# Expert weights by consecutive matrix rows per partition, in chunks of w1 or of w3 alone

## The chip, the cores and the metric

The kernel runs on one core of one Trainium2 chip. The metric is the device time of one execution in microseconds (us). Engines are named as the profile names them: PE is the TensorE matmul, PEld its weight load (the operand that stays in the array), DVE is VectorE, ACT is ScalarE, POOL is GpSimd, SP is SyncE, which here only issues DMAs; SPq and PEq are the sequencers of SP and PE.

## The reference, cut to what matters

An encoder of two layers on 512 tokens of width 1024. Each layer has a mixer (attention in layer 0, a gated recurrence in layer 1), a layer norm, a mixture of 16 experts with two of them chosen per token, and a second layer norm. What the change touches is the mixture:

```
for e in range(16):                       # w1, w3: [16, 1024, 512], w2: [16, 512, 1024], float32
    h = silu(t @ w1[e]) * (t @ w3[e])
    y = y + gates[:, e:e+1] * (h @ w2[e])
```

## The kernel before

**Tiling.** Each expert takes up to 96 tokens (`CAP`). Their rows are gathered from `hbuf` in HBM into `xg` [96, 1024] by an indirect DMA of POOL, two tiles in turn. `x_t` (lines 558 to 569) transposes `xg` on PE by eight blocks of 128 columns; ACT rounds the result to a high part `H` and DVE subtracts for the low part `L`. `w13` (571 to 589) multiplies with w1 and w3 into two PSUM tiles, 48 matmuls of 128x96 by 128x512: for each of the eight blocks `kc` of the contraction the products H·wh, H·wl and L·wh for w1 and for w3, mixed. `glu` (591 to 596) makes `hm` = silu(p1) * p3, with the silu on ACT and the product on DVE. `h_t` (598 to 606) transposes `hm` by four blocks, `w2` (608 to 629) does 24 matmuls, and `scatter` (631 to 638) adds the gated rows to `ybuf` in HBM by an indirect DMA.

**Weights.** Every weight is read from HBM as float32, in chunks of 1 MB, [128, 2048] floats, into rings of tiles named raw, rf, rr and rx (13 tiles while the experts run). A chunk has two parts of 1024 columns. Lines 133 and 134 turn a part into two tiles: ACT casts `wh` = round(w) and DVE subtracts `wl` = w - wh. Such pairs have 6 buffers while the experts run and 4 from the last expert's first part on (line 270). `Stream` (142 to 183) keeps the order: `conv_to(n)` emits conversions up to part n, and the loads before them. `expert_items` (666 to 690) makes the chunks of an expert: four for w1 and w3, each with 256 rows of w1 and the same 256 rows of w3 by two DMAs of 512 KB, and two for w2, of 256 rows each. Row a*128+p of a chunk goes to partition p, so a partition receives two separate rows per DMA, of 2 KB for w1 and w3 and of 4 KB for w2. SP issues all of them.

**Order.** `jobs` (692) runs w13 of expert e and then w2 of expert e-1; `x_t` of expert e+1 stands between them and `h_t` of expert e behind w2. Experts with more than 96 tokens put the rest into blocks of an overflow stage, `overflow` (815 to 834), behind w13 of expert 13, inside a branch whose condition all engines read first. In the profiled execution layer 0 has no such block and layer 1 has one (its tiles end in o: xto, p1o). The last expert's result goes through `direct` and `tail`. Instructions of an engine run in the order in which the program lists them; the framework may move an instruction ahead of others when it builds that list.

Of the kernel before, what the change touches and what calls it, by code (L numbers as in the profile page):

```python
# [8 lines left out]
F32 = mybir.dt.float32  # L9
# [10 lines left out]
P = 128  # L20
D = 1024
KC = D // P
# [6 lines left out]
CAP = 96  # L29
# [20 lines left out]
HALF = 1024  # L50
# [28 lines left out]
def host_consts():  # L79
    c = {}  # L80
    iota1 = np.broadcast_to(np.arange(1, P + 1, dtype=np.float32), (P, P))
    upper = np.triu(np.ones((P, P), np.float32), 1)
    w4 = np.broadcast_to(G - np.arange(G, dtype=np.float32), (P, G))
    tok = np.arange(P, dtype=np.float32)[:, None] + P * np.arange(NT, dtype=np.float32)[None, :]
    ix = np.broadcast_to(np.arange(XBLK, dtype=np.float32), (P, XBLK))
    tm = tok - OOB
    dump = S + np.arange(P, dtype=np.float32)[:, None]
    c["c_h"] = np.concatenate([iota1, upper, tm], 1).astype(np.float16)
    rel = np.arange(-P, P + 1)
    dist = np.abs(rel)  # L90
    far = 7 + sum((dist >= t).astype(np.int64) for t in (8, 12, 16, 23, 32, 46, 64, 91))
    bucket = np.where(rel > 0, 16, 0) + np.where(dist < 8, dist, far)
    rel = (np.arange(32)[:, None] == bucket[None]).astype(np.float32)
    inv = (np.float32(10000.0) ** (-np.arange(16, dtype=np.float32) / np.float32(16))).astype(np.float32)
    ang = np.arange(S, dtype=np.float32)[None, :] * inv[:, None]
    co, si = np.cos(ang), np.sin(ang)
    c["c_rot"] = np.ascontiguousarray(
        np.stack([np.tile(np.concatenate(x, 0), (4, 1)) for x in ((co, co), (-si, si))], 1).astype(np.float32))
    c["c_rel"] = rel
    c["c_sm"] = np.concatenate([np.eye(P, dtype=np.float32), w4, ix, tm, dump], 1).astype(np.float32)  # L100
    return c


def layout(I):
    """The inputs as the kernel loads them: slices, copies and permutations of what came in, and constants."""
    c = host_consts()
    a = {n: np.ascontiguousarray(I[n]) for n in _INS}
    rows = lambda x, n: np.broadcast_to(np.asarray(x).reshape(1, n), (P, n))
    vecs = [np.asarray(I[n]).reshape(-1, P).T for n in VECS]
    rw = np.asarray(I["router_w"]).reshape(KC, P, E).transpose(1, 0, 2).reshape(P, KC * E)  # L110
    a["c_all"] = np.ascontiguousarray(
        np.concatenate([c["c_sm"], rw, rows(I["router_bias"], E), rows(I["l0_sinks"], 8)] + vecs, 1))
    a["c_rel"] = np.ascontiguousarray(np.concatenate([c["c_rel"], np.asarray(I["rel_bias"])], 1))
    a["c_rot"], a["c_h"] = c["c_rot"], c["c_h"]
    a["xt"] = np.ascontiguousarray(np.asarray(I["x"])[0].T)
    w = np.asarray(I["l0_w_in"])
    a["lat"] = np.ascontiguousarray(np.concatenate([w[:, 256:416], w[:, 400:416], w[:, 384:400]], 1))
    a["ukv"] = np.ascontiguousarray(np.asarray(I["l0_w_ukv"]).reshape(P, 8, 2, 64).transpose(0, 2, 1, 3).reshape(P, 1024))
    uq = np.asarray(I["l0_w_uq"]).reshape(2, P, 2, 4, 96)
    uq = np.concatenate([uq[..., a_:z_].reshape(2, P, 2, -1) for a_, z_ in ((0, 64), (64, 96))] +  # L120
                        [np.concatenate([uq[..., 80:96], uq[..., 64:80]], -1).reshape(2, P, 2, -1)], -1)
    a["uq"] = np.ascontiguousarray(uq.transpose(1, 2, 0, 3).reshape(P, 2 * HALF))
    g = np.stack([np.asarray(I["l1_" + n]) for n in ("wa_f", "wx_f", "wa_b", "wx_b")])
    a["gates"] = np.ascontiguousarray(g.reshape(4, 4, 2, P, P).transpose(1, 3, 0, 2, 4).reshape(4, P, HALF))
    return a
# [73 lines left out]
class K:  # L199
# [358 lines left out]
    def x_t(self, xg, nm):  # L558
        nc = self.nc
        H = self.wp.tile([P, KC, CAP], F32R, name="xh" + nm, tag="xh", bufs=1)  # L560
        L = self.wp.tile([P, KC, CAP], F32R, name="xl" + nm, tag="xl", bufs=1)
        for q in range(2):
            pt = self.ps.tile([P, 4, CAP], F32, name=f"xt{nm}{q}", tag="t")
            for j in range(4):
                kc = 4 * q + j
                nc.tensor.transpose(pt[:, j], xg[:, kc * P:(kc + 1) * P], self.ident[:CAP, :CAP])  # L566
            nc.scalar.copy(H[:, 4 * q:4 * q + 4], pt)  # L567
            nc.vector.tensor_tensor(L[:, 4 * q:4 * q + 4], pt, H[:, 4 * q:4 * q + 4].bitcast(F32), op=ALU.subtract)
        return H, L

    def w13(self, st, key, H, L, nm, la):
        nc = self.nc
        p1, p3 = (self.ps.tile([P, 512], F32, name=x + nm, tag="h", bufs=4)[:CAP] for x in ("p1", "p3"))
        for i in range(4):
            a = st.where[(key, "a", i)]
            st.conv_to(a + 2 + la)
            w1h, w1l = st.get(a)
            w3h, w3l = st.get(a + 1)
            for j in range(2):
                kc = 2 * i + j  # L580
                sl = slice(j * 512, (j + 1) * 512)
                f, e = kc == 0, kc == KC - 1
                nc.tensor.matmul(p1, H[:, kc], w1h[:, sl], start=f, stop=False)  # L583
                nc.tensor.matmul(p1, H[:, kc], w1l[:, sl], start=False, stop=False)  # L584
                nc.tensor.matmul(p3, H[:, kc], w3h[:, sl], start=f, stop=False)  # L585
                nc.tensor.matmul(p3, H[:, kc], w3l[:, sl], start=False, stop=False)  # L586
                nc.tensor.matmul(p1, L[:, kc], w1h[:, sl], start=False, stop=e)  # L587
                self.last_mm = nc.tensor.matmul(p3, L[:, kc], w3h[:, sl], start=False, stop=e).ins  # L588
        return p1, p3

    def glu(self, p1, p3, nm):
        nc = self.nc
# [5 lines left out]
    def h_t(self, hm, nm, tag="h"):  # L598
        nc = self.nc
        H, L = (self.wp.tile([P, FC, CAP], F32R, name=f"h{x}{nm}", tag=tag + x, bufs=1) for x in "hl")  # L600
        pt = self.ps.tile([P, FC, CAP], F32, name=f"ht{nm}", tag="t")
        for j in range(FC):
            nc.tensor.transpose(pt[:, j], hm[:, j * P:(j + 1) * P], self.ident[:CAP, :CAP])
        nc.scalar.copy(H, pt)
        nc.vector.tensor_tensor(L, pt, H.bitcast(F32), op=ALU.subtract)  # L605
        return H, L
# [59 lines left out]
    def expert_items(self, it, l, e, what, key):  # L666
        I, nc = self.I, self.nc

        def rows(name, r, n):
            src = I[f"l{l}_{name}"][e] if isinstance(e, int) else \  # L670
                I[f"l{l}_{name}"][bass.ds(e, 1)].rearrange("o a b -> (o a) b")
            return src[r:r + n].rearrange("(a p) b -> p a b", p=P)

        def ld_a(c):
            def load(t):
                for i, n in enumerate(("w1", "w3")):
                    nc.sync.dma_start(t[:, i * HALF:(i + 1) * HALF].rearrange("p (a b) -> p a b", a=2),
                                      rows(n, c * 256, 256))
            return load

        def ld_b(c):
            def load(t):
                nc.sync.dma_start(t.rearrange("p (a b) -> p a b", a=2), rows("w2", c * 256, 256))
            return load

        for c in range(4 if what == "a" else 2):
            if what == "a":
                it.add((key, "a", c), ld_a(c))
            else:
                it.add((key, "w2", c), ld_b(c))  # L690
# [1030 lines left out]
```

## Time and profile before

| | |
|---|---|
| Time, median of 3 runs | 1189.37 us (1189.37 to 1190.99) |
| Profiled execution, first to last instruction (its span) | 1188.6 us |
| PE busy | 1056.6 us (89%) |
| DVE busy | 953.0 us (80%) |
| ACT busy | 768.1 us (65%) |
| Mean granted TensorE clock | 0.937 of full speed |

The profile has no time of its own beside its span; the timed runs stand 0.8 us above it, which is taken as what lies around the span. A busy time is the union of an engine's instructions, and matmuls overlap: one lasts 0.39 us while the next starts 0.23 us after it. So distances between starts say more than durations. The experts run from about 280 to 590 us in layer 0 and from about 841 to 1166 us in layer 1.

### The profile page before, as it was taken

Reading aid. Unit: us, or ns where it says so; the run is one execution under the profiler, and the core shown is the slowest. Engines: PE = TensorE matmul, PEld = TensorE weight load, DVE = VectorE, ACT = ScalarE, POOL = GpSimd, SP = SyncE. Lnnn points to the kernel's source line nnn. Section 1 sums busy time; section 2 is a strip of 40 time slices with the busy share of each in tenths; the row PEclk is TensorE's granted clock in tenths of the full one; section 3 lists DMA queues with packets and bytes.
Section 4 is the critical chain, followed back from the end, with each engine's and each line's share of the span. In section 5 each row is a group of like instructions: output and inputs, shape, how many; then the busy total and the mean of one; then the engine's idle time right before and its main releaser. Section 6 shows DMA issues by size and latency. Waiting matters only on the chain. (4 is left out here: it accounts for less than half of the span.)

```text
span 1188.6 us, 15070 instructions
## 1 busy us (share of the span) xinstructions
PE 1056.6 (89%) x5042; PEld 783.3 (66%) x5042; DVE 953.0 (80%) x1487; ACT 768.1 (65%) x1114; POOL 318.2 (27%) x278
## 2 busy tenths in 40 slices
PE   8999889986999999989789768797799999999892
PEld 6677677874777777756478546586577777776651
DVE  5685878367999999967767999947899998996785
ACT  5455778225788788757526665533578888876762
POOL 1112555125131121111234536203422211210122
PEclk9897999996999999989979969798799999999996
DMA  8180010877999999988713112295799999996983
GB/s 288 54 260 21 2 36 18 335 263 263 324 348 371 360 365 355 345 295 300 188 55 106 35 54 72 87 365 206 269 335 336 380 374 367 387 332 204 335 268 108
DMA packets 132693, 281.25 MB, mean 237 GB/s; under 512 B 8872, under 2 KB 32584, under 8 KB 132480
## 3 DMA queue, kind: packets, MB, share of 16 engines
q1 hardware_dynamic: 121344, 245.20, 56.8%
q0 software_dynamic: 10928, 33.93, 11.9%
q10 hardware_dynamic: 336, 1.08, 0.2%
q8 instruction: 42, 0.69, 0.2%
q14 instruction: 43, 0.35, 0.1%
HBM read 261.41 MB, written 23.74 MB: 240 GB/s over the span
## 5 line engine op out<-in xcount | busy, mean ns | idle before, releaser
L134 DVE TENSOR_TENSOR wl<-rr,wh 128x1024 fp32r<-128x1024 f32 x180 | 212.2, 1218 | 20.9 <-ACT wh L133 20.1
L133 ACT CAST wh<-rr 128x1024 fp32r<-128x1024 f32 x180 | 180.2, 1049 | 39.6 <-PE p L587 34.1
L134 DVE TENSOR_TENSOR wl<-rf,wh 128x1024 fp32r<-128x1024 f32 x104 | 123.8, 1219 | 17.5 <-ACT wh L133 17.3
L133 ACT CAST wh<-rf 128x1024 fp32r<-128x1024 f32 x104 | 105.2, 1048 | 43.4 <-PE p L587 15.1
L134 DVE TENSOR_TENSOR wl<-raw,wh 128x1024 fp32r<-128x1024 f32 (+1 forms) x97 | 116.1, 1225 | 20.2 <-ACT wh L133 11.6
L133 ACT CAST wh<-raw 128x1024 fp32r<-128x1024 f32 (+1 forms) x93 | 92.8, 1031 | 25.5 <-PE p L587 6.0
L636 POOL DMA_INDIRECT ybuf<-y,dst x30 | 57.2, 1907 | 185.7 <-ACT y L635 175.4
L625 PE MATMUL py<-wh,hh 128*96 128x512 f32 x256 | 102.9, 410 | 3.0 <-ACT y L635 1.8
L626 PE MATMUL py<-wl,hh 128*96 128x512 f32 x256 | 102.8, 402 | 1.6 <-DVE wl L134 1.6
L553 POOL DMA_INDIRECT xg<-hbuf,idx x32 | 41.0, 1280 | 236.1 <-PE xt L566 213.2
L583 PE MATMUL p<-wh,xh 128*96 128x512 f32 x256 | 102.8, 401 | 1.4 <-ACT xh L567 1.4
L627 PE MATMUL py<-wh,hl 128*96 128x512 f32 x256 | 102.6, 404 | 0.9 <-DVE hl L605 0.9
L586 PE MATMUL p<-wl,xh 128*96 128x512 f32 x256 | 101.4, 396 | 0.0
L584 PE MATMUL p<-wl,xh 128*96 128x512 f32 x256 | 101.4, 396 | 0.0
L585 PE MATMUL p<-wh,xh 128*96 128x512 f32 x256 | 101.1, 395 | 0.3
L588 PE MATMUL p<-wh,xl 128*96 128x512 f32 x256 | 101.1, 395 | 0.0
L587 PE MATMUL p<-wh,xl 128*96 128x512 f32 x256 | 100.7, 393 | 0.0
L134 DVE TENSOR_TENSOR wl<-rx,wh 128x1024 fp32r<-128x1024 f32 x56 | 66.1, 1219 | 7.6 <-ACT wh L133 7.6
L133 ACT CAST wh<-rx 128x1024 fp32r<-128x1024 f32 x56 | 56.2, 1050 | 9.9 <-PE p L587 7.6
L625 PEld LDWEIGHTS py<-wh,hh 128*96 128x96 f32 x256 | 42.1, 166 | 25.0 <-issue 4.9
L918 PE MATMUL pom<-wh,x 128*128 128x512 f32 x128 | 52.2, 408 | 4.4 <-DVE ge L1089 4.4
L627 PEld LDWEIGHTS py<-wh,hl 128*96 128x96 f32 x256 | 42.5, 166 | 19.8 <-DVE hl L605 1.8
(410 smaller groups left out, 2600.2 us busy)
## 6 DMA issues: line engine op xcount, KB each, us to landing
rr<-l_w SPq DMA_DIRECT2D x124, 512.0 KB, 11.2
rf<-l_w SPq DMA_DIRECT2D x68, 512.0 KB, 13.0
rr<-l_w SPq DMA_DIRECT2D x28, 1024.0 KB, 13.6
rx<-l_w SPq DMA_DIRECT2D x36, 512.0 KB, 10.6
raw<-l_w SPq DMA_DIRECT2D x36, 512.0 KB, 12.9
rf<-l_w SPq DMA_DIRECT2D x15, 1024.0 KB, 13.0
raw<-l_w SPq DMA_DIRECT2D x13, 1024.0 KB, 6.5
raw<-l_w_in SPq DMA_DIRECT2D x11, 1024.0 KB, 5.5
```

The source lines that it names most:

```text
L133: nc.scalar.copy(h[:, :w], r[:, a:a + w])
L134: (nc.gpsimd if lp else nc.vector).tensor_tensor(l[:, :w], r[:, a:a + w], h[:, :w].bitcast(F32), op=ALU.subtract)
L583: nc.tensor.matmul(p1, H[:, kc], w1h[:, sl], start=f, stop=False)
L584: nc.tensor.matmul(p1, H[:, kc], w1l[:, sl], start=False, stop=False)
L585: nc.tensor.matmul(p3, H[:, kc], w3h[:, sl], start=f, stop=False)
L586: nc.tensor.matmul(p3, H[:, kc], w3l[:, sl], start=False, stop=False)
L587: nc.tensor.matmul(p1, L[:, kc], w1h[:, sl], start=False, stop=e)
L588: self.last_mm = nc.tensor.matmul(p3, L[:, kc], w3h[:, sl], start=False, stop=e).ins
L625: nc.tensor.matmul(py[n], H[:, c], a, start=c == 0, stop=False)
L626: nc.tensor.matmul(py[n], H[:, c], b, start=False, stop=False)
L627: nc.tensor.matmul(py[n], L[:, c], a, start=False, stop=c == FC - 1)
L636: nc.gpsimd.indirect_dma_start(out=self.ybuf[l], out_offset=bass.IndirectOffsetOnAxis(ap=dst, axis=0), in_=y, in_offset=None, bounds_check ...
```

## The change

A chunk holds 512 rows of w1 alone or of w3 alone, in turn, by one DMA of 1 MB; partition p receives the four consecutive rows 4p to 4p+3, which are 8 KB in one piece in HBM. A chunk of w2 still has 256 rows, but partition p receives rows 2p and 2p+1, again 8 KB in one piece. Bytes, chunks, parts, conversions, matmuls and transposes stay the same in number; an expert has six weight DMAs in place of ten.

The contraction index is permuted to match: block kc of a half now holds the columns 4p+a of x, so the transposes of `x_t` read `xg` with a distance of four floats (16 bytes) between columns, and those of `h_t` read `hm` with a distance of two floats (8 bytes). In `w13` a part belongs to w1 or to w3 alone, and its six matmuls run together, L·wh as the third of each block; `conv_to` is called for each part and not for each chunk. p1 is complete twelve matmuls before p3.

```diff
     def x_t(self, xg, nm):
+        x4 = xg.rearrange("s (c p a) -> s c p a", c=2, a=4)
...
-                nc.tensor.transpose(pt[:, j], xg[:, kc * P:(kc + 1) * P], self.ident[:CAP, :CAP])
+                nc.tensor.transpose(pt[:, j], x4[:, kc // 4, :, kc % 4], self.ident[:CAP, :CAP])
...
     def w13(self, st, key, H, L, nm, la):
...
-            st.conv_to(a + 2 + la)
-            w1h, w1l = st.get(a)
-            w3h, w3l = st.get(a + 1)
-            for j in range(2):
-                kc = 2 * i + j
-                sl = slice(j * 512, (j + 1) * 512)
-                f, e = kc == 0, kc == KC - 1
-                nc.tensor.matmul(p1, H[:, kc], w1h[:, sl], start=f, stop=False)
-                nc.tensor.matmul(p1, H[:, kc], w1l[:, sl], start=False, stop=False)
-                nc.tensor.matmul(p3, H[:, kc], w3h[:, sl], start=f, stop=False)
-                nc.tensor.matmul(p3, H[:, kc], w3l[:, sl], start=False, stop=False)
-                nc.tensor.matmul(p1, L[:, kc], w1h[:, sl], start=False, stop=e)
-                self.last_mm = nc.tensor.matmul(p3, L[:, kc], w3h[:, sl], start=False, stop=e).ins
+            for half in range(2):
+                st.conv_to(min(a + half + 2, st.where[(key, "a", 3)] + 2) + la)
+                wh, wl = st.get(a + half)
+                for j in range(2):
+                    kc = 4 * (i // 2) + 2 * half + j
+                    p, sl = ps[i % 2], slice(j * 512, (j + 1) * 512)
+                    nc.tensor.matmul(p, H[:, kc], wh[:, sl], start=kc == 0, stop=False)
+                    nc.tensor.matmul(p, H[:, kc], wl[:, sl], start=False, stop=False)
+                    self.last_mm = nc.tensor.matmul(p, L[:, kc], wh[:, sl], start=False, stop=kc == KC - 1).ins
...
     def h_t(self, hm, nm, tag="h"):
...
+        h4 = hm.rearrange("s (c p a) -> s c p a", c=2, a=2)
-            nc.tensor.transpose(pt[:, j], hm[:, j * P:(j + 1) * P], self.ident[:CAP, :CAP])
+            nc.tensor.transpose(pt[:, j], h4[:, j // 2, :, j % 2], self.ident[:CAP, :CAP])
...
     def expert_items(self, it, l, e, what, key):
-            return src[r:r + n].rearrange("(a p) b -> p a b", p=P)
+            return src[r:r + n].rearrange("(p a) b -> p (a b)", p=P)
...
-                for i, n in enumerate(("w1", "w3")):
-                    nc.sync.dma_start(t[:, i * HALF:(i + 1) * HALF].rearrange("p (a b) -> p a b", a=2),
-                                      rows(n, c * 256, 256))
+                nc.sync.dma_start(t, rows(("w1", "w3")[c % 2], c // 2 * 512, 512))
...
-                nc.sync.dma_start(t.rearrange("p (a b) -> p a b", a=2), rows("w2", c * 256, 256))
+                nc.sync.dma_start(t, rows("w2", c * 256, 256))
```

## Rows read from the trace of the kernel before

**Rows 1.** The page, busy tenths in 40 slices of the span, granted clock, DMA.
```profile
PE   8999889986999999989789768797799999999892
...
PEclk9897999996999999989979969798799999999996
DMA  8180010877999999988713112295799999996983
```

**Rows 2.** Windows: us, busy us (instructions) by engine, clock, DMA share, GB/s.
```profile
core 0: us, PE busy (x) PEld busy (x) DVE busy (x) ACT busy (x) POOL busy (x), PEclk, DMA share, GB/s
320.00:520.00 200.00, 200.00 (x969) 143.07 (x968) 185.54 (x228) 164.32 (x203) 39.43 (x26) 1.00 1.00 345
535.00:575.00 40.00, 38.14 (x168) 25.50 (x166) 29.52 (x32) 27.90 (x35) 8.29 (x9) 1.00 0.80 260
1109.00:1152.00 43.00, 41.13 (x184) 27.66 (x182) 35.01 (x38) 32.64 (x42) 8.97 (x8) 1.00 0.93 312
```

**Rows 3.** Waits from 320 to 520 us: us in total, times, longest.
```profile
ACT wh L133 <- PE p L587: 20.4, 27, 0.8
...
DVE wl L134 <- DMA rf<-l_w: 0.2, 1, 0.2
```

**Rows 4.** Waits of SP's queue over the span.
```profile
SPq L677 <- DVE wl L134: 170.1, 71, 14.5
...
SPq L677 <- DMA rr<-l_w: 23.4, 34, 1.2
```

**Rows 5.** Timeline of PE in one expert of layer 0: start, us, what.
```profile
414.91 0.40 PE L588 MATMUL p<-wh,xl 128*96 128x512 f32 x1
415.14 0.82 PE L566 MATMUL xt<-call,xg 96*128 96x96 f32 x8
415.75 0.46 PE L625 MATMUL py<-wh,hh 128*96 128x512 f32 x1
...
421.35 0.49 PE L603 MATMUL ht<-call,hm 96*128 96x96 f32 x4
421.62 0.45 PE L583 MATMUL p<-wh,xh 128*96 128x512 f32 x1
```

**Rows 6.** Instructions of lines 566, 603, 583, 918: ns min/median/max.
```profile
L566 PEld LDWEIGHTS xt<-call,xg x256: 137/140/231, 280.7 to 1126.8; 96*128 96x128 f32 x128
...
L566 PEld LDWEIGHTS xto<-call,xg x8: 138/142/143, 1082.8 to 1083.5; 96*128 96x128 f32 x8
...
L603 PEld LDWEIGHTS ht<-call,hm x128: 138/141/224, 297.1 to 1153.3; 96*128 96x128 f32 x128
...
L583 PEld LDWEIGHTS p<-wh,xh x256: 159/161/277, 282.2 to 1150.0; 128*96 128x96 f32 x128
...
L918 PEld LDWEIGHTS pom<-wh,x x128: 186/188/333, 200.8 to 820.8; 128*128 128x128 f32 x128
```

**Rows 7.** DVE reductions of lines 437 (contiguous) and 441 (16 bytes apart): ns.
```profile
L437 DVE TENSOR_REDUCE rg<-rw x4: 197/242/290, 262.4 to 831.2; 128x12 f32<-128x144 f32 x2, 128x4 f32<-128x48 f32 x2
...
L441 DVE TENSOR_REDUCE rw<-rw x4: 200/258/314, 263.0 to 832.9; 128x48 f32<-128x144 f32 x2, 128x16 f32<-128x48 f32 x2
```

**Rows 8.** Timeline of PE where it stands still: layer 0's start, layer 1's end.
```profile
294.77 0.82 PE L566 MATMUL xt<-call,xg 96*128 96x96 f32 x8
296.30 0.47 PE L583 MATMUL p<-wh,xh 128*96 128x512 f32 x1 [0.71 <-ACT xh L567]
...
1117.45 0.39 PE L583 MATMUL p<-wh,xh 128*96 128x512 f32 x1
1117.99 0.47 PE L585 MATMUL p<-wh,xh 128*96 128x512 f32 x1
...
1126.89 0.71 PE L625 MATMUL py<-wh,hh 128*96 128x512 f32 x2
1128.41 0.47 PE L626 MATMUL py<-wl,hh 128*96 128x512 f32 x1 [0.81 <-DVE wl L134]
...
1135.08 0.47 PE L625 MATMUL py<-wh,hh 128*96 128x512 f32 x1 [0.92 <-ACT y L635]
```

**Rows 9.** Timeline, PE and SP at layer 0's first gather.
```profile
277.40 0.88 SPq L677 DMA_DIRECT2D rf<-l_w  x2
...
280.74 1.51 PE L566 MATMUL xt<-call,xg 96*128 96x96 f32 x8 [5.93 <-DMA xg<-hbuf,idx]
```

**Rows 10.** The page, SP's queue: packets, MB, share of 16 engines' span.
```profile
q1 hardware_dynamic: 121344, 245.20, 56.8%
```

More of the change, by code (lines that the diff above doesn't have):

```diff
@@ L572, in w13 @@
         nc = self.nc
-        p1, p3 = (self.ps.tile([P, 512], F32, name=x + nm, tag="h", bufs=4)[:CAP] for x in ("p1", "p3"))
+        ps = [self.ps.tile([P, 512], F32, name=x + nm, tag="h", bufs=4)[:CAP] for x in ("p1", "p3")]
         for i in range(4):
             a = st.where[(key, "a", i)]
-            st.conv_to(a + 2 + la)
-            w1h, w1l = st.get(a)
-            w3h, w3l = st.get(a + 1)
-            for j in range(2):
-                kc = 2 * i + j
-                sl = slice(j * 512, (j + 1) * 512)
-                f, e = kc == 0, kc == KC - 1
-                nc.tensor.matmul(p1, H[:, kc], w1h[:, sl], start=f, stop=False)
-                nc.tensor.matmul(p1, H[:, kc], w1l[:, sl], start=False, stop=False)
-                nc.tensor.matmul(p3, H[:, kc], w3h[:, sl], start=f, stop=False)
-                nc.tensor.matmul(p3, H[:, kc], w3l[:, sl], start=False, stop=False)
-                nc.tensor.matmul(p1, L[:, kc], w1h[:, sl], start=False, stop=e)
-                self.last_mm = nc.tensor.matmul(p3, L[:, kc], w3h[:, sl], start=False, stop=e).ins
-        return p1, p3
+            for half in range(2):
[7 more added lines that the diff above has]
+                    self.last_mm = nc.tensor.matmul(p, L[:, kc], wh[:, sl], start=False, stop=kc == KC - 1).ins
+        return ps
     def glu(self, p1, p3, nm):
```

## The prediction

> **What bounds the kernel now.** I read the page's slices first, to see which engine is full where the change works. From the eighth slice on the experts run, PE stands at nine tenths and the DMA row at nine tenths beside it [rows 1]; either could set the end, and the change touches both. The windows split them: from 320 to 520 us PE is busy all 200 us at full clock, DVE 185.54, the DMA share is 1.00 [rows 2]. Two full resources need a third view, the waits. In those 200 us the longest wait of the conversion is that of ACT's cast for PE to give a buffer back, 20.4 us in 27 times, while the only wait of a conversion for a weight DMA is 0.2 us, once [rows 3]. SP's queue says the same from its side: it stands 170.1 us for DVE to free a ring tile, and 23.4 us for DMAs [rows 4]. The weights come early and wait; PE sets the pace of the experts, and the DMA row is full because DMA follows PE. The timeline of PE is then read for distances: matmuls start 0.23 us apart, eight transposes take 415.75 - 415.14 = 0.61 us, 76 ns each, and four take 0.27 us, 68 ns each [rows 5]. An expert is 72 x 0.23 + 0.61 + 0.27 = 17.4 us of PE with no gap. Whatever lengthens a PE instruction there lengthens the kernel; whatever hastens a load there does not.
>
> **The change part by part.** The sum is made on the profiled span of 1188.6 us, with the 0.8 us around it that the median shows.
>
> Weight DMAs (fewer, larger, in one piece per partition): 0. They are covered by the ring: loads wait for tiles, not tiles for loads [rows 3, 4]. If the cover were gone, the price would be a wait of ACT's cast for a DMA; a gain can't be more than the 0.2 us now lost to one. SP issues four DMAs fewer per expert, and what is queued behind them are only more loads that wait for tiles.
>
> Matmuls of `w13`: 0. As many, of the same shape, and `w2` already runs three in a row into one PSUM tile at the same 0.23 us [rows 5].
>
> Transposes of `x_t`: the dear part. The operand that the change makes strided is the one loaded into the array, 96 partitions by 128 columns. That load takes 140 ns, whereas the ordinary loads take 161 ns for 96 columns and 188 ns for 128 [rows 6]. So ordinary loads pay 27 ns for 32 columns, 0.84 ns a column, above a fixed 80 ns; the transposing load pays (140 - 80)/128 = 0.47 ns a column, 60 ns in all. These 60 ns hide under the 76 ns from transpose to transpose [rows 5]. No row shows a load with columns 16 bytes apart. Below, the price is nothing: a load may grow by 16 ns before it is seen at all. Above, the nearest row with words 16 bytes apart is DVE's reduction: from 48 to 144 words it grows from 200 to 314 ns, 1.19 ns a word, against 0.97 ns for adjacent words (197 to 290) [rows 7]. A load at 1.19 ns a column needs 152 ns, 76 more than the distance now. Between these ends I take the ordinary pace of PE's own loads, 0.84 ns: 107 ns, 31 more than 76. It is a row of the same unit, and a read that takes a word every 0.47 ns, twice as fast as any DVE row, is the one with most to lose from a scattered pattern. The first of eight loads is made under a matmul of 0.23 us, so seven of eight pay: 0.22 us per `x_t`. There are 256 + 8 such transposes, 33 sets [rows 6]: 33 x 0.22 = +7.2 us, with the ends 0 and 33 x 7 x 76 ns = 17.6 us.
>
> DVE's ratio 1.19/0.97 = 1.23 is the row against this: the load would grow from 60 to 74 ns and stay hidden under 76, and the sum would lose its one large term. [...]
>
> Transposes of `h_t`: 132 of them in 33 sets, columns 8 bytes apart, three of four paying. The ends are 0 and 33 x 3 x 76 ns = 7.5 us. I take 0, since half of the reads stay neighbours and a load may grow by 8 ns unseen under its 68 ns.
>
> Part-by-part matmuls and conversions. A buffer pair comes free after six matmuls and not after twelve, which matters only where PE stands still. Beyond the distances above that is 0.89 us at a layer's second expert (it waits for ACT's `xh`, which stands behind a silu) and, behind the overflow stage, 0.31 us (a late cast), 1.06 us (`wl`) and 1.08 us (the evacuation `y`) [rows 8]; both layers show the same four, 3.3 us each. The 1.06 us stays: that `wl` is queued on DVE behind the product of `glu`, which waits for p3, and p3 does not end sooner. The 1.08 us waits for ACT's `y` of an earlier `w2`, which is not moved. The other two, 1.2 us a layer, may go, because p1 ends twelve matmuls earlier, and with it ACT's silu. I take half, -1.2 us for both layers. Against it, L·wh is now the third matmul of a block and not the fifth, 0.46 us sooner; behind the second expert's `x_t` the low part is barely ready, and I take +0.25 us a layer. Together -0.7, ends -6.6 and +2.
>
> DMAs of other queues. The weight packets take 0.568 x 16 x 1188.6 us / 121344 = 89 ns each [rows 10]; 8 KB at that pace is four times as much, 356 ns. Gathers share the engines and take turns. Only a layer's first gather is waited for, PE standing 5.93 us, with two loads issued beside it [rows 9]. Six of its 4 KB rows per engine, each behind a packet 267 ns longer, is 1.6 us at most a layer; the few loads make that rare. I take +0.3 us a layer, +0.6, ends 0 and 3.2.
>
> Sum: 0 + 0 + 7.2 + 0 - 0.7 + 0.6 = +7.1 us. 1188.6 + 7.1 + 0.8 = 1196.5 us, forecast as **1196.5**.
>
> **The rivals.** *Strided loads hidden, nothing else moves.* For it DVE's ratio [rows 7] and the 16 ns of slack [rows 5, 6]; against it that the load is already the fastest reader here. Its sum is -0.1: 1189.3 us, and with the small terms' ends 1187 to 1191.7. Chance 0.23.
>
> *The stalls go: faster.* One mechanism: buffer pairs return singly, so casts and silu run earlier where lead is short, behind the overflow stage and at the layers' starts. Its place is the four gaps of rows 8, its price 3.3 us a layer, at most 6.6. It decides only if the strided load stays below 76 ns; then two thirds of it give 1189.4 - 4.4 = 1185 us. For it: these windows have PE idle 1.9 us in 40 and in 43 [rows 2]. Against it: two of the four gaps hang on instructions that don't move. Chance 0.20.
>
> *The dearer stride.* The load goes at DVE's 1.19 ns a column: +17.6 for `x_t`, and up to +7.5 if `h_t` is caught too. That gives 1189.4 + 17.6 = 1207, to 1214. For it, only that DVE reads so slowly [rows 7]; against it, PE's own slow pace is 0.84. Chance 0.10.
>
> *The permutation does not pay because DMA was never late* is part of the forecast, not a rival: nothing in the sum comes from the packets.
>
> **How the numbers follow.** The forecast (strided load near PE's ordinary pace) has the other 0.47; its own range, from a third of the price to 12 us, is 1192 to 1201. Slower by over 0.2% (2.4 us, about what the spread of 1189.37 to 1190.99 lets one tell) is the forecast and the dearer stride, 0.57; within it 0.23; faster 0.20. The range must hold 8 in 10: it reaches down to the middle of the faster case, 1185, and up to the dearer stride, 1208.
>
> **What the profile after would show.** Step by step: the load of line 566's successor at about 188 ns and not 140, eight transposes at about 0.83 us and not 0.61, `h_t` still at 140 and 0.27; the distance of matmuls 0.23 us as now; an expert at 17.6 to 17.9 us; PE still busy 200 of 200 us from 320 to 520; weight packets fewer and a lower DMA share, with SP's queue still waiting for DVE. I am wrong if the load stays at 140 ns (then the time falls to the first two rivals), if the load exceeds 200 ns (the third), or if PE shows new waits for ACT or DVE in the middle of the experts, which would mean that the new order of conversions, not the stride, set the time.

## The result and the profile after

The changed kernel takes **1199.33 us** (median of 4 runs, 1198.59 to 1199.62); the kernel before took 1189.37 in the same session. The ratio is 1.0095, with a 95% interval of 1.0066 to 1.0124: slower by 10 us between the medians, by 11 us by the ratio. The forecast was 1196.5, slower, within 1185 to 1208. The profiled execution has a span of 1197.4 us, 8.8 more than before. Executions of one kernel differ: in 35 runs beside the last experiments the kernel before took from 1179.86 us (mean granted clock 0.947) to 1190.62 (0.937), so single profiles are compared stage by stage below, and times by their intervals.

First the transposes, whose loads the prediction made the dear part. The instructions of lines 567 and 601 (566 and 603 before), ns min/median/max, answer to [rows 6] (here and below `...` stands for lines left out):

```profile
L567 PEld LDWEIGHTS xt<-call,xg x256: 195/220/231, 278.5 to 1135.8; 96*128 96x128 f32 x128
...
L601 PEld LDWEIGHTS ht<-call,hm x128: 194/216/221, 295.4 to 1162.4; 96*128 96x128 f32 x128
```

Both loads grew from 140 ns to about 220. What that costs is read as distances in the timeline of PE (start, us, what), which answers to [rows 5]; the last three lines are from the end of layer 1's last expert:

```profile
415.73 0.40 PE L585 MATMUL p<-wh,xl 128*96 128x512 f32 x1
415.97 1.09 PE L567 MATMUL xt<-call,xg 96*128 96x96 f32 x8
416.84 0.45 PE L623 MATMUL py<-wh,hh 128*96 128x512 f32 x1
...
422.43 0.60 PE L601 MATMUL ht<-call,hm 96*128 96x96 f32 x4
422.82 0.45 PE L583 MATMUL p<-wh,xh 128*96 128x512 f32 x1
...
1159.83 0.40 PE L585 MATMUL p<-wh,xl 128*96 128x512 f32 x1
1162.05 0.72 PE L601 MATMUL ht<-call,hm 96*128 96x96 f32 x4 [1.82 <-DVE hm L592]
1163.34 0.47 PE L623 MATMUL py<-wh,hh 128*96 128x512 f32 x1 [0.57 <-ACT hh L602]
```

Eight transposes of `x_t` take 416.84 - 415.97 = 0.87 us (0.61 before), four of `h_t` 0.39 (0.27 before). A strided load of 220 ns appears every 0.87/8 = 109 ns, so each load overlaps the next, and what is paid is less than the load's growth. Matmuls still start 0.23 us apart. The last lines show something new: `h_t` of the last expert stands 1.82 us for the product `hm`, where the kernel before stood 0.85:

```profile
1153.04 0.55 PE L603 MATMUL ht<-call,hm 96*128 96x96 f32 x4 [0.85 <-DVE hm L595]
```

PE is full in the middle of the experts as before. The windows (us, busy us and instructions of PE, PEld, DVE, ACT and POOL, clock, DMA share, GB/s; compare [rows 2]) and the waits from 320 to 520 us (us, times, longest; compare [rows 3]):

```profile
320.00:520.00 200.00, 200.00 (x949) 145.27 (x948) 183.93 (x224) 166.18 (x199) 37.12 (x26) 1.00 0.97 354
535.00:575.00 40.00, 38.60 (x170) 26.61 (x169) 32.60 (x35) 29.58 (x37) 6.86 (x8) 0.99 0.68 228
```

```profile
ACT wh L133 <- PE p L585: 12.9, 40, 0.4
...
ACT wh L133 <- PE py L625: 10.5, 25, 1.7
...
ACT wh L133 <- DMA rr<-l_w: 0.9, 3, 0.3
```

PE is busy 200 of 200 us in both kernels, with 949 matmuls recorded where there were 969. Conversions still wait for PE, and next to nothing for DMA. The packets did change, as the page shows (SP's queue answers to [rows 10]):

```profile
DMA packets 71443, 281.22 MB, mean 235 GB/s; under 512 B 6760, under 2 KB 30472, under 8 KB 45888
...
q1 hardware_dynamic: 60096, 245.19, 53.7%
```

71443 - 45888 = 25555 packets have 8 KB or more. On SP's queue half as many packets as before carry the same bytes, at 53.7% of the engines' span in place of 56.8%; a packet takes 0.537 x 16 x 1197.4 / 60096 = 171 ns in the mean, against 89.

### The profile page after: what moved, and what is told of

Its sections match the earlier page's. It is cut to its first block, busy times and chain, and to the rows that moved or that the text cites. A ratio compares the mean times of both kernels' runs of the same rounds, so it can differ in the third digit from the quotient of the medians.

```text
span 1197.4 us, 14745 instructions
## 1 busy us (share of the span) xinstructions
PE 1068.0 (89%) x5042; PEld 797.9 (67%) x5042; DVE 957.7 (80%) x1487; ACT 780.6 (65%) x1114; POOL 314.7 (26%) x278
## 2 busy tenths in 40 slices
DMA packets 71443, 281.22 MB, mean 235 GB/s; under 512 B 6760, under 2 KB 30472, under 8 KB 45888
## 3 DMA queue, kind: packets, MB, share of 16 engines
q1 hardware_dynamic: 60096, 245.19, 53.7%
q10 hardware_dynamic: 336, 1.08, 0.2%
## 5 line engine op out<-in xcount | busy, mean ns | idle before, releaser
L134 DVE TENSOR_TENSOR wl<-rr,wh 128x1024 fp32r<-128x1024 f32 x180 | 215.1, 1227 | 22.1 <-ACT wh L133 20.8
L133 ACT CAST wh<-rr 128x1024 fp32r<-128x1024 f32 x180 | 184.8, 1050 | 42.2 <-PE p L585 25.0
L133 ACT CAST wh<-rf 128x1024 fp32r<-128x1024 f32 x104 | 107.1, 1048 | 44.8 <-DMA rf<-l_w_out 13.9
L553 POOL DMA_INDIRECT xg<-hbuf,idx x32 | 43.4, 1357 | 254.6 <-PE xt L567 207.9
L584 PEld LDWEIGHTS p<-wl,xh 128*96 128x96 f32 x512 | 83.6, 163 | 37.5 <-DVE wl L134 3.4
L583 PEld LDWEIGHTS p<-wh,xh 128*96 128x96 f32 x512 | 84.3, 165 | 35.4 <-ACT xh L568 1.3
L585 PEld LDWEIGHTS p<-wh,xl 128*96 128x96 f32 x512 | 83.4, 163 | 36.0
L634 POOL DMA_INDIRECT ybuf<-y,dst x30 | 45.9, 1530 | 176.0 <-ACT y L633 124.0
```

Source lines behind the costliest of these rows:

```text
L133: nc.scalar.copy(h[:, :w], r[:, a:a + w])
L134: (nc.gpsimd if lp else nc.vector).tensor_tensor(l[:, :w], r[:, a:a + w], h[:, :w].bitcast(F32), op=ALU.subtract)
L553: self.last_gather = self.nc.gpsimd.indirect_dma_start(out=xg, out_offset=None, in_=self.hbuf[0:n], in_offset=bass.IndirectOffsetOnAxis(ap ...
L583: nc.tensor.matmul(p, H[:, kc], wh[:, sl], start=kc == 0, stop=False)
L584: nc.tensor.matmul(p, H[:, kc], wl[:, sl], start=False, stop=False)
L585: self.last_mm = nc.tensor.matmul(p, L[:, kc], wh[:, sl], start=False, stop=kc == KC - 1).ins
```

## The experiments

The theory: the strided loads of the two transposes cost all of the loss, 0.26 + 0.11 us per set. The main rivals: the rows or the order of parts cost it; the loads are covered.

**1. Both reads made contiguous again, the rest of the change kept.**

```diff
-  nc.tensor.transpose(pt[:, j], x4[:, kc // 4, :, kc % 4], ...)
+  nc.tensor.transpose(pt[:, j], xg[:, kc * P:(kc + 1) * P], ...)
-  nc.tensor.transpose(pt[:, j], h4[:, j // 2, :, j % 2], ...)
+  nc.tensor.transpose(pt[:, j], hm[:, j * P:(j + 1) * P], ...)
```

> The changed kernel with both transposing reads put back to 128 adjacent columns; 8 KB rows, 1 MB transfers, chunks and order stay. It leaves out the matching of the contraction index, so its output is another one. Theory (the strided weight loads cost all of the loss): the loads of xt and ht fall from about 0.22 to 0.14 us, eight transposes of xt from 0.87 to 0.61 us and four of ht from 0.39 to 0.28, over 33 sets 8.6 + 3.6 = 12.2 us less: about 1187 us. Rival (the new rows or the new order of parts cost the time, the loads are covered): it stays within 2 us of 1199.

Measured: 1188.77 us, ratio to the kernel before 1.0025 (1.0009 to 1.0041). Loads are back at 146 and 141 ns in the mean, the distances at 0.61 and 0.28 us. Most of the loss went with the stride. About 3 us stayed, which the theory had no place for.

**2. The strided reads alone, in the kernel before.**

```diff
-  nc.tensor.transpose(pt[:, j], xg[:, kc * P:(kc + 1) * P], ...)
+  nc.tensor.transpose(pt[:, j], xg.rearrange("s (c p a) -> s c p a", c=2, a=4)[:, kc // 4, :, kc % 4], ...)
   (and hm likewise with a=2)
```

> The kernel before with the strided transposing reads alone; rows of 2 and 4 KB, transfers and order stay as they were. It leaves out the matching of the contraction index, so its output is another one. Theory (the strided weight loads cost the loss): 8.6 + 3.6 = 12.2 us more than before, about 1201 us. Rival (rows or order cost it): within 2 us of the kernel before, 1189.

Measured: 1243.52 us, ratio 1.0497 (1.0471 to 1.0523): far outside both. The groups of PE's loads (busy us, mean ns, idle before) name the reason:

```profile
L566 PEld LDWEIGHTS xtl<-call,xg 96*128 96x128 f32 x8 | 1.3, 221 | 11.3 <-issue 11.3
L566 PEld LDWEIGHTS xto<-call,xg 96*128 96x128 f32 x8 | 1.1, 214 | 0.1
```

`xtl` exists only in the loop over further overflow blocks: with layer 0 computed otherwise, layer 1's routing overfilled a second block. From `xto` to the next `x_t` this run takes 69.88 us, against 25.07 before: 44.8 us of other work. The total says nothing of the stride. The steady experts do: nine sets take 162.00 us in layer 0, against 158.64, so 0.37 us a set, which is the theory's.

**3. The rows of before, with the chunks, transfers and order of the change.** Against experiment 1 this differs in the packets, and in the output, since the contraction index is matched again; both have one overflow block, in layer 1, and their steady sets agree (table at the end of this section).

```diff
-  src[r:r + n].rearrange("(p a) b -> p (a b)", p=P)
+  src[r:r + n].rearrange("(a p) b -> p a b", p=P)
   (the loads' tiles viewed to match, and contiguous reads as in experiment 1)
```

> The changed kernel with the rows of before: pieces of 2 and 4 KB and contiguous transposing reads, with the chunks of w1 or w3 alone, 1 MB transfers and part-by-part order of the change. Against the kernel with contiguous reads and 8 KB rows it differs in the packets alone. Theory (the packets are worth nothing, since no wait ended on a weight transfer): the same as that one within 2 us, about 1187 us. Rival (8 KB packets gave back part of the loss): 3 us or more slower than that one, 1190 or above.

Measured: 1188.93 us beside 1188.77, ratio 1.0036 (1.0022 to 1.005); once more on another chip, beside the later experiments:

> Old rows and contiguous reads with the chunks and order of the change, once more, beside the kernels with the moved casts on one chip. Theory: ratio to the kernel before 1.0036 as measured first, granted clock 0.79 over the second matrix of both last experts.

1188.92 us, ratio 1.0033 (1.0012 to 1.0054), clock 0.78 over the second matrix of the two last experts. The 8 KB packets are worth nothing here: 59136 packets more or less on SP's queue, the time the same within 0.2 us. The DMA share of 1.00 in [rows 2] looks like a kernel that DMA binds, and the waits of [rows 3, 4] say that it isn't.

**4. Other distances of the columns.** The kernel before, with the read of `x_t` at 8, 16 or 32 bytes, or adjacent, by the expert's number modulo 4 (lines 570, 572, 574, 576).

```diff
+  xa = lambda a: xg.rearrange("s (c p a) -> s c p a", p=P, a=a)[:, kc // a, :, kc % a]
+  e % 4 == 0: xa(2)    1: xa(4)    2: xa(8)    else: as before
```

> The kernel before with the distance of the columns in the transposing read of xt set by the expert: 8 bytes for a quarter of the experts, 16 bytes, 32 bytes, and adjacent for the rest and the overflow; it leaves out the matching of the contraction index. Theory (any distance but adjacent costs the same): the three strided loads take 0.22 us each and eight transposes 0.87 us, adjacent ones 0.14 and 0.61. Rival (a read costs by how many columns share 16 bytes): 8 bytes takes 0.14 to 0.18 us, 16 bytes 0.22, and 32 bytes 0.22 or more.

The groups of PE's loads (busy us, mean ns, idle before):

```profile
L570 PEld LDWEIGHTS xt<-call,xg 96*128 96x128 f32 x64 | 9.2, 214 | 12.3 <-issue 11.7
L572 PEld LDWEIGHTS xt<-call,xg 96*128 96x128 f32 x64 | 9.0, 215 | 0.9
L574 PEld LDWEIGHTS xt<-call,xg 96*128 96x128 f32 x64 | 8.2, 203 | 2.7 <-PEq L839 2.0
L576 PEld LDWEIGHTS xt<-call,xg 96*128 96x128 f32 x64 | 6.2, 141 | 1.3
```

214, 215, 203 and 141 ns; eight transposes take 0.86, 0.87, 0.81 and 0.61 us. Nearly the theory: each of the three distances costs, and 32 bytes costs a little less than 16. The rival falls. The run itself took 1183.59 us, below most of the kernel before's although it pays for strided loads; the end of this section comes back to it.

**5. One cast of `w2` moved behind `hm`, in the changed kernel**, at the last expert of each layer and in the overflow block: the new wait of 1.82 us.

```diff
-  st.conv_to(min(a + half + 2, st.where[(key, "a", 3)] + 2) + la)
+  st.conv_to(min(a + half + 2 + la, st.where[(key, "a", 3)] + 2
+                 + (0 if key in ("o", (key[0], E - 1)) else la)))
```

What stands before `hm` in the changed kernel is seen on DVE, and why it is late on ACT (timelines):

```profile
1159.04 2.36 DVE L134 TENSOR_TENSOR wl<-rr,wh 128x1024 fp32r<-128x1024 f32 x2 [1.65 <-ACT wh L133]
1161.32 0.68 DVE L592 TENSOR_TENSOR hm<-hm,p 96x512 f32<-96x512 f32 x1
```

```profile
1157.48 0.59 ACT L591 ACTIVATE hm<-p 96x512 f32<-96x512 f32 x1 [1.73 <-PE p L585]
1157.97 3.87 ACT L133 CAST wh<-rr 128x1024 fp32r<-128x1024 f32 x4
```

p1 ends before p3 now: silu runs at 1157.48, and p3 is complete at 1160.23. On DVE two `wl` come ahead of `hm`; their casts stand behind that silu on ACT, so the two end only at 1161.40. In the kernel before, silu stands ahead of the same casts, but DVE takes `hm` first:

```profile
1152.30 0.68 DVE L595 TENSOR_TENSOR hm<-hm,p 96x512 f32<-96x512 f32 x1 [2.41 <-PE p L588]
1152.91 2.35 DVE L134 TENSOR_TENSOR wl<-rr,wh 128x1024 fp32r<-128x1024 f32 x2
```

So what changed is DVE's order. Why the list of instructions came out in this order was not looked into.

> The changed kernel, in which at the last expert of each layer and in the overflow block one cast of w2 less is issued ahead of the product hm on VectorE (one wl then stands before hm in place of two, and hl comes one wl earlier). Theory (hm waits behind two wl conversions there, since silu, which now ends earlier, holds the casts of w2 back on ScalarE): the gap before these three h_t falls from about 2.0 to 0.9 us, 3 us less in all, about 0.25% under the changed kernel run beside it. Rival (the wait is covered by what follows, or another wait takes its place, the wl of the second part): within 1 us of the changed kernel.

Measured: 1195.58 us, ratio 1.0055 (1.004 to 1.0071), against 1200.03 for the changed kernel beside it (experiment 8): 4.4 us less, 0.4%. The three gaps are 0.78 us each, 1.05 less. The theory's sign and place are right, its size too small. What the profiles show beside the gaps is the overflow block's second matrix: 6.61 us at a granted clock of 1.00, against 8.19 and 8.90 at 0.79 and 0.66 in the two profiles of the changed kernel.

**6. Experiment 2 in layer 1 alone**, so that the routing stays.

```diff
+  ... if nm.lstrip("o")[0] == "1" else <contiguous>
```

> The kernel before with both strided transposing reads in layer 1 alone, so that the routing, which follows from layer 0, stays that of the kernel before. The contraction index is not matched in layer 1, so its output is another one. Theory: 0.266 us more for eight transposes of x_t and 0.11 for four of h_t, over 17 sets 6.4 us, ratio 1.0054 to the kernel before. Rival (a large part is covered elsewhere): under 3 us, ratio below 1.0025.

Measured: 1193.52 us, ratio 1.0047 (1.0028 to 1.0066), +5.6 us. The interval, 3.3 to 7.8 us, holds the theory's 6.4 as well as the 5.6; it shuts out the rival's "under 3 us" only just. Nine steady sets take 162.12 us against 158.67, in full what the theory says. But from `xto` to the last `py`, where three of the 17 transposes of `x_t` and four of `h_t` lie, it is 79.18 against 79.15: the set between the overflow block and the last expert pays 0.4 us, and the last second matrix, in which `py` no longer waits for `hl`, gives 0.66 back. There PE waits for casts and products anyhow, and a later transpose waits less.

**7. Experiment 3 with the moved cast of experiment 5.**

> The kernel with old rows and contiguous reads, but the chunks and order of the change, with the same move of one cast behind hm at the last experts and in the overflow block. Theory (the order of parts costs about 4 us against the kernel before, 3 of them in these waits, 1.1 in the parts' matmuls): within 1.5 us of the kernel before, ratio 1.0000 to 1.0013. Rival (the 4 us lie elsewhere): ratio 1.003 or more as without the move.

Measured: 1182.65 us, ratio 0.9948 (0.9928 to 0.9968): faster than the kernel before, more than either theory gave. Again on another chip:

> The same with one cast of w2 moved behind hm at the last experts and in the overflow block, once more. Theory (the shorter gap keeps the granted clock at 1.00 over the second matrix of the last experts, where the others fall to 0.79, 1.5 us each): ratio to the kernel before 0.995, 6 us or more under the kernel without the move. Rival (its first ratio was chance): 1.000 to 1.002, 3 us under the kernel without the move.

1182.09 us, ratio 0.9981 (0.9962 to 0.9999), 6.8 us under experiment 3 beside it. The time came out again, and the distance to experiment 3 is the theory's; the ratio lies between the theory's 0.995 and the rival's 1.000. The gap is the shorter one, and the wait for `hl` is left (timeline of PE, second run):

```profile
1145.84 0.55 PE L601 MATMUL ht<-call,hm 96*128 96x96 f32 x4 [0.78 <-DVE hm L592]
1146.96 0.47 PE L623 MATMUL py<-wh,hh 128*96 128x512 f32 x1 [0.57 <-ACT hh L602]
...
1148.58 0.47 PE L625 MATMUL py<-wh,hl 128*96 128x512 f32 x1 [0.45 <-DVE hl L603]
```

Three gaps shorter by 1.05 us are 3.1 of the 6.8 us. Most of the rest is, in these profiles, the clock. The windows over the second matrix of layer 1's last expert, the changed kernel first, then this one, then experiment 4:

```profile
1163.34:1170.78 7.44, 7.31 (x25) 4.71 (x25) 1.87 (x3) 0.68 (x1) 0.00 (x0) 0.77 1.06 208
```

```profile
1146.96:1153.29 6.33, 5.88 (x24) 3.89 (x25) 3.17 (x4) 1.58 (x2) 1.30 (x2) 1.00 1.02 199
```

```profile
1148.78:1155.12 6.34, 5.89 (x25) 3.90 (x25) 4.30 (x5) 2.52 (x3) 1.21 (x2) 1.00 1.03 202
```

That the shorter gap keeps the clock, as the theory has it, is not shown. Experiment 4 has the end of the kernel before, with its gap of 0.85 us and its wait of 0.45 us for `hl`, and its clock stayed at 1.00; the profile of the kernel before fell to 0.78 behind the same waits.

**8. The changed kernel once more, beside 5 to 7.**

> The changed kernel itself again, beside the others on one chip, for the ratio to the kernel before with a narrower interval. Theory: 12.2 us for the strided loads and 4 us for the order of parts, less what the mixers vary by: ratio 1.011 to 1.014. Rival (the first four runs were typical): 1.0095 or less.

Measured: 1200.03 us, ratio 1.0093 (1.0064 to 1.0121), the first result again, as the rival had it, and under the theory's 1.011. The sum 12.2 + 4 counted sets whose cost is covered (experiment 6 shows it for layer 1).

**9. Experiment 7 with `hl` one conversion earlier** on DVE at the same places.

```diff
+  if key in ("o", (key[0], E - 1)):
+      st.conv_to(st.where[(key, "w2", 0)] + 2)
+      with self.tc.issue_after(self.last_hl):
+          st.conv_to(i + 1 + la)
   st.conv_to(i + 1 + la)
```

> The kernel with the moved cast, in which at the same three places hl also comes one conversion earlier on VectorE, before the wl of the third part of w2. Theory: the wait of 0.45 us for hl goes at three places, about 1.3 us less than the kernel with the moved cast alone, clock 1.00 there. Rival (the wl that now comes after hl is late in its turn): the same time within 1 us.

Measured: **1179.81 us, ratio 0.9952 (0.9935 to 0.9969)**, 2.3 us under experiment 7 beside it, where the theory gave 1.3; the two intervals just overlap. In the profiles `py` is 0.69 us shorter at each of the three places (6.33 to 5.64 at the last experts), 2.1 us. DVE now stands as meant (timeline), and `py` has no wait after its first:

```profile
1142.19 1.22 DVE L134 TENSOR_TENSOR wl<-rr,wh 128x1024 fp32r<-128x1024 f32 x1 [1.64 <-ACT wh L133]
1143.42 0.68 DVE L592 TENSOR_TENSOR hm<-hm,p 96x512 f32<-96x512 f32 x1
1144.02 1.22 DVE L134 TENSOR_TENSOR wl<-rr,wh 128x1024 fp32r<-128x1024 f32 x1
1145.25 0.56 DVE L603 TENSOR_TENSOR hl<-ht,hh 128x384 fp32r<-128x384 f32 x1
```

**10. The same aim in the kernel before, with its own order.**

```diff
+  with self.tc.issue_after(<the last cast of w2's first chunk>):
       nc.scalar.activation(hm, p1, AF.Silu)
   (and the conversions of w2's second chunk after hl, as in 9)
```

> The kernel before, with its own rows and order of parts; at the last experts and in the overflow block the casts of the first chunk of w2 come ahead of silu on ScalarE, and hl ahead of the next conversions on VectorE. Theory (the gain of the moved cast does not need the order of parts of the change, only a short gap there): the wait for hl goes, the granted clock stays at 1.00 over the second matrix, 3 to 5 us under the kernel before, ratio 0.996 to 0.9975. Rival (the casts, which wait for buffers, now hold silu and hm back): the gap before h_t grows and the time is the same or 1 to 3 us longer.

Measured: 1182.95 us, ratio 0.9981 (0.9964 to 0.9998). The gap before `h_t` grew from 0.85 to 1.12 us at the two last experts, as the rival said, yet the wait for `hl` went, the clock stood at 1.00, and the kernel gained 2.7 us, less than the theory's 3 to 5. So the gain doesn't hang on the order of parts. Experiment 9 beside it is 3.1 us faster, but only 1.4 us of this lie in the experts' stages of the two profiles; the rest lies outside the experts, where both do the same work.

The second matrix of the last experts, by kernel (gap before `h_t`, time from the first `py` matmul to the first of `pd`, granted clock in it; layer 0 and layer 1), and that of the overflow block up to the next `x_t`:

| kernel | gap, us | `py`, us | clock | overflow: us, clock |
|---|---|---|---|---|
| before | 0.85, 0.85 | 7.88, 7.85 | 0.78, 0.78 | 6.78, 1.00 |
| changed | 1.83, 1.82 | 7.20, 7.44 | 0.76, 0.77 | 8.19, 0.79 |
| 3, first run | 1.82, 1.82 | 7.85, 7.25 | 0.78, 0.76 | 6.79, 1.00 |
| 3, second run | 1.82, 1.82 | 7.73, 7.89 | 0.78, 0.78 | 8.61, 0.68 |
| 4 | 0.85, 0.85 | 6.32, 6.34 | 1.00, 1.00 | 6.78, 1.00 |
| 5 | 0.78, 0.78 | 7.59, 7.22 | 0.78, 0.76 | 6.61, 1.00 |
| 7, second run | 0.78, 0.78 | 6.33, 6.33 | 1.00, 1.00 | 6.78, 1.00 |
| 9 | 0.77, 0.78 | 5.64, 5.63 | 1.00, 1.00 | 6.09, 1.00 |
| 10 | 1.13, 1.12 | 5.77, 5.75 | 1.00, 1.00 | 6.22, 1.00 |

Rows "before" and 4 have the same gap before `h_t` and another clock, and so have the two rows of 3 in the overflow block (1.82 us in both). So part of what the clock gives back in experiments 7, 9 and 10 may be the luck of their profiles; their times, from 8 to 12 runs each, don't hang on one profile.

And the stages, us between starts of PE's instructions (nine steady sets: from the layer's fourth `x_t` to its thirteenth; the columns 1, 3 and 9 are experiments; in the rows up to the first `x_t` and between the layers the kernels do the same work; the last row runs in each layer from the first `x_t` to the first `pd`):

| stage | before | changed, two profiles | 1 | 3, two profiles | 9 |
|---|---|---|---|---|---|
| to the first `x_t` | 280.7 | 278.5, 275.7 | 276.6 | 278.4, 278.8 | 279.0 |
| layer 0, nine steady sets | 158.64 | 162.36, 162.36 | 159.06 | 159.06, 159.06 | 159.06 |
| between the layers, `pd` to `x_t` | 256.5 | 252.6, 254.7 | 255.0 | 255.6, 255.0 | 252.7 |
| layer 1, nine steady sets | 158.67 | 162.24, 162.24 | 158.82 | 158.82, 158.82 | 158.82 |
| `xto` to the next `x_t` | 25.07 | 27.87, 29.78 | 28.18 | 26.08, 28.18 | 22.77 |
| to layer 1's last `py` | 54.08 | 54.89, 55.01 | 54.37 | 53.76, 54.37 | 51.03 |
| experts of both layers | 624.7 | 639.6, 640.6 | 630.2 | 627.1, 630.3 | 619.2 |

## Why the prediction was right, and where its steps were not

The sign and the main mechanism were right: PE sets the pace, the strided load surfaces, and nothing is to be had from the packets. The total came out 3 us low, from errors of both signs; that it is no further off is in part luck. One of the prediction's own signs of being wrong was met: the load exceeds 200 ns, which was to mean the dearer stride, 1207 us. The load's duration was the wrong thing to watch, since loads overlap; the distance between transposes, 109 ns, is the forecast's 107 and not the dearer stride's 152. An expert takes 18.04 us (162.36 / 9), not 17.6 to 17.9.

*What bounds the kernel, and the weight DMAs at 0.* Shown: experiments 1 and 3 differ in the packets, and take the same time. The 23.4 us of [rows 4] are one row of SP's waits for DMAs; with the other rings the experts' loads wait 65 us for DMAs, against 288 us for DVE's `wl`, and the reading stands.

*The 0.8 us around the span.* It is 1.8 us wherever a run has both figures (1199.21 against 1197.4 in the changed kernel). By that the profile before would be of an execution of about 1190.4 us and not of the median. The forecast's difference of 7.1 us doesn't change by it.

*`x_t`, +7.2.* That the strided load surfaces is right, and the size is a little low: a set pays 0.266 us, 33 ns for each of eight, 8.8 us over 33 sets if all pay, where 31 ns for seven of eight were expected. How the size was worked out is not confirmed. The split into a fixed 80 ns that hides and a part per column that shows would give 188 ns for a load at 107 ns a piece; the load is 220 ns, and by the same split (220 - 80 = 140) the distance would be 140 ns, not 109. What a load hides under its neighbours is 64 ns for adjacent columns (140 - 76) and 111 ns for strided ones (220 - 109). So the near hit of the distance is luck, and what sets it is open.

*`h_t`, 0.* This step was wrong. "Half of the reads stay neighbours" was the reason, an estimate with no row behind it, and nothing of the kind is seen: 216 ns at 8 bytes, 219 and 220 at 16 (medians). At 32 bytes the load of `x_t` gets shorter and not longer (206 ns median, experiment 4). The stride costs `h_t` 0.11 us per set, 3.6 us if all pay. The upper end, 7.5, held it.

*The 33 sets.* Not all pay. In the profile of experiment 6 the nine steady sets of layer 1 pay in full, and the stretch with the overflow block and the last experts is no longer than before. The times alone (5.6 us, between 3.3 and 7.8) could not tell this from 6.4.

*Part-by-part order, -0.7.* Wrong in sign. With contiguous reads it costs 3 to 4 us by the ratios of experiments 1 and 3, and 2.3 to 5.5 us in the experts' stages of their three profiles. The step that failed is where it looked: at the four gaps of [rows 8] alone. In sum these did what was forecast, which is luck again, since one by one they did not. These lines are from the changed kernel, the same places as the last of [rows 8]:

```profile
1126.90 0.48 PE L584 MATMUL p<-wl,xh 128*96 128x512 f32 x1 [0.67 <-DVE wl L134]
...
1135.98 0.45 PE L623 MATMUL py<-wh,hh 128*96 128x512 f32 x1
1136.26 0.39 PE L624 MATMUL py<-wl,hh 128*96 128x512 f32 x1
...
1142.87 0.48 PE L623 MATMUL py<-wh,hh 128*96 128x512 f32 x1 [0.68 <-ACT hh L602]
```

The 1.06 us for `wl`, which were to stay, are gone; the 0.31 us grew to 0.84 (the distance to the matmul before is 1.07 us, not 0.54); the 1.08 us fell to 0.84. With the gap at the second expert, 0.2 us shorter in experiment 1, and a new one of 0.2 us, this is some 0.7 us less a layer. What the prediction left out is larger: three gaps before `h_t`, at the last experts and in the overflow block, where DVE now puts two `wl` ahead of `hm`, 1 us each; about 1 us in 33 sets (from the first matmul of `w13` to the next `x_t` 11.195 us in layer 0 and 11.164 in layer 1, against 11.148 in the kernel before); and 0.5 to 0.8 us at each layer's opening, which was not followed further. In two of the three profiles the clock in the overflow block adds almost 2 us. The rival "the stalls go" got its four gaps smaller but not its gain: that came only when conversions were moved at the other three places (experiments 7 and 9).

*Other queues' DMAs, +0.6.* Not seen: PE stands 6.00 us for layer 0's first gather, 5.93 before [rows 9].

The parts as measured: by the ratios 8.1 us for the strided loads (1.0093 - 1.0025 of 1187 us, experiment 8 against 1) and 3.0 for the order, which make up the whole by construction. In the experts' stages of the profiles they are 9.4 to 10.4 and 2.3 to 5.5, and the whole is 14.9 and 15.9; the rest of the span, where both kernels do the same work, was 563.9 us in the profile before and 557.8 and 557.1 in those of the changed kernel. Where the 4 us between the two counts lie stays open. What the prediction left out, +3 for the order, and what it undercounted at `h_t`, +2 or more, are larger than its miss of 3 us, because sets under cover pay nothing.

The version to keep is experiment 9: the order of parts with old rows and contiguous reads, and both conversions out of the way. It is 1.4% under the changed kernel by the two ratios (0.9952 / 1.0093, from two chips) and 0.5% under the kernel before.

## What to carry to other kernels

A permutation that is free in DMA (0.2 us between experiments 1 and 3) has to be undone somewhere; see whether the engine that undoes it is the one that sets the pace, since a transpose from a strided operand took PE a third to 0.43 as much again at the three distances tried. A DMA share of 1.00 is no proof that DMA binds [rows 2, 3]: follow the waits from the conversion to its releaser before you pay for larger packets. A load's duration is not its cost where loads overlap (220 ns each, one every 109 ns): read the distances. When an accumulation ends earlier, look at the order of what is queued around its readers; and where a layer has one expert that nothing overlaps, the order of two conversions there was worth more (9.1 us from the second run of experiment 3 to experiment 9) than the layout of 200 MB of weights.

## What the runs showed of the hardware that was not expected

A load into the array of 96 x 128 fp32 took 140 ns from adjacent columns, 214 to 220 at 8 and 16 bytes, 203 to 206 at 32 (means and medians), and eight in a row came out every 76, 108, 109 and 101 ns (adjacent, 8, 16, 32 bytes): of these distances none is much cheaper than another, and all cost more than adjacent columns. The granted clock over 24 matmuls after the last `h_t` was 0.78 in the kernel before and 1.00 in experiments 4, 7, 9 and 10, with matmuls 0.43 us apart for part of the first and 0.23 throughout the others: 7.9 us against 6.3 in experiment 4 for the same work behind the same waits (0.85, 0.57 and 0.45 us). The gap alone doesn't decide: in experiment 10 the clock stayed at 1.00 behind 1.12 us, with no later wait for `hl`, and in experiment 5 it stood at 0.78 and 0.76 behind 0.78 us, with strided loads. What does was not settled, and it is not the kernel alone. The stretch up to the first `x_t` varied from 275.7 to 280.7 us between profiles, though no expert runs in it. A difference of 2 us in the total needs its interval, and so does one in a stage that PE waits in: `xto` to the next `x_t` took 26.1 and 28.2 us in two profiles of experiment 3, whose nine steady sets agree within 0.01 us.
